# A two-block transformer kernel on one core: the way from the first layer norm into the experts is rewritten

## The chip, the cores and the metric

One core of a Trainium2 chip runs the whole program in one launch. The metric is the device time of one execution in microseconds (us). Engines: PE multiplies matrices (PEld is its weight load), DVE and ACT do elementwise work, POOL is a slower elementwise engine, and SP only issues DMA transfers. Each engine runs its own instructions in order; semaphores tie them together.

## What is computed

Two stacks of two layers each over 256 tokens of width 1024, all in float32. A layer of the first stack is token mixing (three branches with gates), a layer norm, a mixture of 16 experts of which each token uses two, and a second layer norm. Only the piece between the mixing and the experts, and the first expert pair, are touched:

```python
x = layer_norm(DN_ALPHA * x + mix, ln1_g[l], ln1_b[l])
ffn = moe(x.reshape(B * S, D), w_router, router_bias, w1[l], w3[l], w2[l])
x = layer_norm(DN_ALPHA * x + ffn, ln2_g[l], ln2_b[l])
# route: scores = sigmoid(x2 @ w_router); two experts of the best group of four per token;
# gate weight = the two scores, divided by their sum
# an expert: h = silu(xb @ w1[e]) * (xb @ w3[e]);  y = h @ w2[e]
```

The second stack (attention of three kinds and a feed-forward layer) isn't touched.

## The kernel before

The 256 tokens lie as two tiles of 128 partitions (b = 0, 1), each 1024 wide and worked on as two halves of 512 (h = 0, 1). Experts are taken in eight pairs (p = 0 to 7); an expert has 64 slots (CAP), and a one-hot matrix (`sel`) made from each token's rank gathers tokens into slots by matmul. The weights stream through a ring of slots of 1 MB: a pair takes four slots each of w1, w3 and w2, each slot two transfers of 512 KB. `pair_weights` issues them on SP in program order, and a transfer starts when its slot is free and the last one on its semaphore has landed.

The way in, per layer (`first_mix`, end, and `moe`, beginning): `residual` adds the mixing result and takes statistics; `columns` transposes x on PE for the router; `logits` multiplies by router weights into which the norm is folded; `ln_stats` (L503 on) makes mean and `rs` = (var + eps)^-0.5, with both steps after `bn_aggr` on POOL. The norm is applied in three steps per half tile: `center` on DVE, `scale` on ACT, `add` on POOL. `route` turns the logits into scores (tanh on ACT), picks experts in a chain of some twenty small DVE instructions that ends in the mask `rsel` (L855), and counts ranks on PE. `scaled` starts the accumulators of the expert output with ALPHA * x on PE. `gate_weights` normalises the gates after the ranks.

The first pair's gather takes x itself, in float32, with every second column as one weight load, so that the columns match w1 and w3 as they were loaded: partition p holds rows 2p and 2p+1, in one run of 4 KB. The other pairs gather from `xs`: x in three bfloat16 thirds, made by `thirds` (L959 on) after the branch: ACT writes a third, DVE subtracts it from x, three rounds for two tiles. ACT reads x in order there and writes at a step of 256 bytes.

Between the first gather and the first pair's matmuls stands a branch (`tc.If(n > CAP)`, L1058): a path for experts with more than 64 tokens, which this input doesn't take. Every engine loads the largest count and jumps over the path's code. `tc.mark_branch_hint_location` names no engines here, and the built program holds no hint.

What sets the order: PE, DVE and ACT keep the written order between `order.__enter__()` in `first_mix` and `order.__exit__` before the branch, and PE keeps it again through the eight pairs. What stands outside, as `thirds` and `rows_of`, is placed by the scheduler where it fits; it puts the first round of `thirds` on ACT ahead of the branch.

Of the kernel before, what the change touches and what calls it, by code (L numbers as in the profile page):

```python
# [20 lines left out]
NB = 2  # L21
# [19 lines left out]
class Kernel:  # L41
# [458 lines left out]
    def ln_stats(self, st, b):  # L500

        nc = self.nc
        if b == 0:  # L503
            self.mv = self.t(self.cp, [P, NB, 2], F32, "bmv", 2)
            self.rs = self.t(self.cp, [P, NB], F32, "brs", 2)
        mv, rs = self.mv[:, b], self.rs[:, b:b + 1]
        nc.vector.bn_aggr(mv, st)
        nc.gpsimd.tensor_scalar(mv[:, 1:2], mv[:, 1:2], 1e-5, None, OP.add)
        nc.gpsimd.tensor_tensor(rs, mv[:, 1:2], self.half, OP.pow)
        return mv[:, 0:1], rs  # L510

# [32 lines left out]
    def first_mix(self, l, x, mem):  # L544
# [97 lines left out]
        def halves(h, b):  # L642
            return x[:, b, h * 512:h * 512 + 512]
# [19 lines left out]
            nc.vector.scalar_tensor_tensor(halves(h, b), halves(h, b), norms[b][0],  # L663
                                           g[:, h * 512:h * 512 + 512], OP.subtract, OP.mult)

        def scale(h, b):
            nc.scalar.activation(halves(h, b), halves(h, b), AF.Copy, scale=norms[b][1])

        def add(h, b):
            nc.gpsimd.tensor_tensor(halves(h, b), halves(h, b), bb[:, h * 512:h * 512 + 512], OP.add)  # L670

        pss, = self.dense_tok((mh, ml), [ws[0]])
        for b in range(NB):
# [5 lines left out]
        with tc.high_priority(offset=300):  # L679
            residual(1, 0, pss[0])  # L680
            columns(1, 0)
            norms.append(self.ln_stats(st[0], 0))
            for h in range(2):
                center(h, 0)
                scale(h, 0)
                add(h, 0)
        acc = [self.psd() for _ in range(4)]

        def scaled(b, h):
# [4 lines left out]
        order.__enter__()  # L694
        residual(1, 1, pss[1])
        logits(0, 0)
        logits(0, 1)
        columns(1, 1)
        norms.append(self.ln_stats(st[1], 1))
        logits(1, 0)  # L700
        logits(1, 1)
        for h in range(2):
            center(h, 1)
        scaled(0, 0)
        scale(0, 1)
        add(0, 1)
        lgs = self.t(self.cp1, [P, NB, NE], F32, "logits", 1)
        for b in range(NB):
            nc.vector.scalar_tensor_tensor(lgs[:, b], lg[:, b], norms[b][1], self.wb[:, l], OP.mult, OP.add)
        self.M_.__exit__(None, None, None)  # L710
        self.wp_.__exit__(None, None, None)
        return list(pre.values()), (acc, lgs), (scale, add, scaled), order

    def value_weights(self, l):

# [30 lines left out]
    def pair_weights(self, l, p, part, n):  # L746


        w = self.I[part]
        r = self.slot()  # L750
        for a in range(2):
            rows = w[l, 2 * p + a]
            self.nc.sync.dma_start(r[:, a], rows[n * P:(n + 1) * P].rearrange("p (k f) -> p k f", k=2)
                                   if part == "w2" else
                                   rows[2 * n * P:2 * (n + 1) * P].rearrange("(p k) f -> p k f", k=2))
        return r

    def expert_weights(self, l, p, part):
# [62 lines left out]
    def route(self, logits, E, aside):  # L821

        nc = self.nc
        sh = [P, NB, NE]
        sc = self.t(E, sh, F32, "rsc", 1)
        nc.scalar.activation(sc, logits, AF.Tanh, scale=0.5)
        aside()
        bi = self.t(E, sh, F32, "rbi", 1)
        nc.vector.scalar_tensor_tensor(bi, sc, 0.5, self.rbias[:, None, :].to_broadcast(sh),
                                       OP.mult, OP.add)  # L830

        b4 = bi.rearrange("p b (g e) -> p (b g) e", g=4)
        pr = self.t(E, [P, NB * 4, 6], F32, "rpr", 1)
        nc.vector.tensor_tensor(pr[:, :, 0:3], b4[:, :, 0:3], b4[:, :, 1:4], OP.add)
        nc.vector.tensor_tensor(pr[:, :, 3:5], b4[:, :, 0:2], b4[:, :, 2:4], OP.add)
        nc.vector.tensor_tensor(pr[:, :, 5:6], b4[:, :, 0:1], b4[:, :, 3:4], OP.add)
        gs, best = self.gs, self.best
        nc.vector.tensor_reduce(gs[:, :, 0:4], pr.rearrange("p (b g) e -> p b g e", b=NB), AX.X, OP.max)
        nc.vector.tensor_reduce(best[:, :, 0:1], gs[:, :, 0:4], AX.X, OP.max)
        for b in range(NB):  # L840
            nc.vector.match_replace(gs[:, b], best[:, b], gs[:, b], -NEG)

        g4 = bi.rearrange("p b (g e) -> p b g e", g=4)
        for b in range(NB):
            nc.vector.scalar_tensor_tensor(g4[:, b], gs[:, b, 0:4, None].to_broadcast([P, 4, 4]), NEG,
                                           g4[:, b], OP.add, OP.add)
        m8 = [self.t(E, [P, 8], F32, "rm8", 2) for _ in range(NB)]
        for b in range(NB):
            nc.vector.max(m8[b], bi[:, b])
        for b in range(NB):  # L850
            nc.vector.memset(m8[b][:, 2:8], 1.0e30)
        for b in range(NB):
            nc.vector.match_replace(bi[:, b], m8[b], bi[:, b], -3.0e38)
        sel = self.t(E, sh, BF16, "rsel", 1)
        nc.vector.tensor_scalar(sel, bi, -2.0e38, None, OP.is_lt)  # L855

        pk = self.psa()
        nc.tensor.matmul(pk[:, 0:16], self.tri, sel[:, 0], start=True, stop=True)
        nc.tensor.matmul(pk[:, 16:32], self.ones, sel[:, 0], start=True, stop=False)
        nc.tensor.matmul(pk[:, 16:32], self.tri, sel[:, 1], start=False, stop=True)  # L860
        nc.tensor.matmul(pk[:, 32:48], self.ones, sel[:, 0], start=True, stop=False)
        nc.tensor.matmul(pk[:, 32:48], self.ones, sel[:, 1], start=False, stop=True)
        rk = self.t(E, sh, F32, "rrk", 1)
        nc.vector.scalar_tensor_tensor(rk, pk[:, 0:32].rearrange("p (b e) -> p b e", b=NB), 1.0, sel,
                                       OP.add, OP.mult)
        return sc, sel, rk, pk

    def gate_weights(self, sc, sel, pk, E):
        nc = self.nc
        sh = [P, NB, NE]  # L870
        most = self.t(E, [P, 1], F32, "rmost", 1)
        nc.vector.tensor_reduce(most, pk[:, 32:48], AX.X, OP.max)
        most_i = self.t(E, [P, 1], I32, "rmosti", 1)
        nc.vector.tensor_copy(most_i, most)
        nc.vector.tensor_scalar(sc, sc, 0.5, 0.5, OP.mult, OP.add)
        G = self.t(E, sh, F32, "rG", 1)
        nc.vector.tensor_tensor(G, sc, sel, OP.mult)
        gsum = self.t(E, [P, NB], F32, "rgsum", 1)
        nc.vector.tensor_reduce(gsum, G, AX.X, OP.add)
        nc.vector.reciprocal(gsum, gsum)  # L880
        nc.vector.tensor_tensor(G, G, gsum[:, :, None].to_broadcast(sh), OP.mult)
        return G, most_i

    def overflow(self, l, x, acc, rk, G, E):

# [33 lines left out]
    def moe(self, l, x, pre):  # L919
# [5 lines left out]
        self.R3_ = tc.tile_pool(name=f"raw3_{l}", bufs=1, reuse_waits="tile")  # L925
        self.R3 = self.R3_.__enter__()
        with tc.tile_pool(name=f"moe{l}", bufs=1, reuse_waits="tile") as E:
            pre, (acc, logits), (scale, add, scaled), order = pre
            def aside():

                scale(1, 1)
                add(1, 1)
                scaled(0, 1)
                scaled(1, 0)

            sc, sel, rk, pk = self.route(logits, E, aside)

            def slots(p, dt=BF16):

# [18 lines left out]
            def thirds():  # L958

                xs = self.t(E, [P, 3, NB, 8, P], BF16, "xs", 1)  # L960
                for i in range(3):
                    for b in range(NB):
                        to = xs[:, i, b].rearrange("p (n k) c -> p n c k", k=2)
                        xb = x[:, b].rearrange("p (n c k) -> p n c k", k=2, c=P)
                        nc.scalar.copy(to, xb)  # L965
                        if i < 2:
                            nc.vector.tensor_tensor(xb, xb, to, OP.subtract)
                return [lambda b, k, i=i: xs[:, i, b, k] for i in range(3)]

            def rows_of():  # L970

                t = self.t(E, [P, NB, 7, NE], BF16, "rt", 1)
                nc.vector.memset(t[:, :, 1:4], 0.0)
# [3 lines left out]
                nc.vector.tensor_tensor(rest, G, t[:, :, 4], OP.subtract)  # L977
                nc.vector.tensor_copy(t[:, :, 5], rest)
                nc.vector.tensor_tensor(t[:, :, 6], rest, t[:, :, 5], OP.subtract)
                id16 = self.t(E, [P, P], BF16, "id16", 1)  # L980
                nc.scalar.copy(id16, self.ident)
                ps = self.psa()
# [63 lines left out]

            mT = mv = None
            label = f"few{l}"
            tc.mark_branch_hint_location(label, "LikelyTaken")
            s = slots(0, F32)  # L1050
            scaled(1, 1)
            xk = x.rearrange("p b (n c k) -> p b n k c", k=2, c=P)
            g_ = gather(s, [lambda b, k: xk[:, b, k // 2, k % 2]])
            order.__exit__(None, None, None)
            G, most = self.gate_weights(sc, sel, pk, E)
            nxt = [self.expert_weights(l, 1, n) for n in ("w1", "w3")]
            n = nc.values_load(most[0:1, 0:1], min_val=0, max_val=S)
            with tc.If(n > CAP, label=label):  # L1058
# [5 lines left out]
            for p in range(8):  # L1064
# [8 lines left out]
                    g, bb = self.ln_rows(I["ln2_g"][l], I["ln2_b"][l])  # L1073
                sl = hidden(w, g_)
                if p == 0:
                    rows, pick = rows_of()
                if p < 7:
                    g_ = gather(slots(p + 1), parts)
                elif l < DEPTH - 1:
                    mT = self.mem_T(mem)  # L1080
                sT, gsl = back(p)
# [553 lines left out]
```

## Time and profile before

| | us |
|---|---|
| Three runs | 1663.26, 1670.53, 1671.15 (median 1670.53) |
| The profiled execution, its own time | 1663.95 |
| Its span in the trace | 1662.2 |
| PE busy | 1589.8 (96%) |
| DVE, ACT, POOL busy | 869.2, 741.2, 105.9 |

PE is busy nearly throughout, so the whole follows PE: what counts is where PE stands idle, and how fast it goes where its clock isn't granted in full. DVE and ACT are busy half the time, and matter where PE waits for them.

### The profile page before, as it was taken

How to read it: one execution, taken by the hardware profiler on the slowest of the kernel's cores; microseconds unless marked ns; L12 is line 12 of the kernel's file. 1: busy time of each engine (PE TensorE's matmuls, PEld its weight loads, DVE VectorE, ACT ScalarE, POOL GpSimd, SP SyncE). 2: the span in 40 equal slices, each digit the busy share in tenths (PEclk: the TensorE clock that was granted, in tenths of full speed). 3: DMA queues.
4: the chain of work that ended last, by engine and by line, in shares of the span. 5: the costliest groups of instructions: out<-in, count | busy, mean ns of one | idle time of the engine just before them, and what ended most of it. 6: DMA issues, size and time to landing. Idle time of an engine off the chain costs nothing.

```text
span 1662.2 us, 24843 instructions
## 1 busy us (share of the span) xinstructions
PE 1589.8 (96%) x9844; PEld 1191.6 (72%) x9844; DVE 869.2 (52%) x1778; ACT 741.2 (45%) x1186; POOL 105.9 (6%) x141
## 2 busy tenths in 40 slices
PE   7999999799999999999799998989999999899999
PEld 7877998434345987998444443866989987688897
DVE  5586547311123688547421213777655568775554
ACT  5546445610103555544710102656555556655553
POOL 0000013000000000012100000130000000200000
PEclk9999999899999999999899999999999999999999
DMA  9553867699999653686699998623555554145551
GB/s 309 178 171 102 324 235 250 248 372 409 409 408 376 204 165 117 257 299 228 223 377 409 409 409 326 236 93 104 170 185 175 180 163 168 52 161 194 178 184 45
DMA packets 158470, 394.78 MB, mean 238 GB/s; under 512 B 15716, under 2 KB 21860, under 8 KB 158340
## 3 DMA queue, kind: packets, MB, share of 16 engines
q1 hardware_dynamic: 153088, 384.98, 63.6%
q0 software_dynamic: 2144, 6.91, 1.3%
q8 instruction: 80, 1.31, 0.3%
q10 hardware_dynamic: 3108, 1.16, 0.3%
q14 instruction: 50, 0.41, 0.1%
HBM read 391.97 MB, written 1.05 MB: 236 GB/s over the span
## 4 chain that ended last, share of the span: by engine, by line
PE 41%; DVE 4%; ACT 2%; POOL 1%; DMA 1%; issue 1%; ACTq 0%; DVEq 0%; POOLq 0%
PE a L1010 6%; PE d L113 6%; PE d L112 6%; PE d L111 6%; PE a L111 4%; PE a L112 4%; PE a L113 4%; PE a L1031 3%; DMA raw<-in_w_in_dram 1%; PE a L954 1%; DVE wl L105 1%; ACT xs L965 1%; PE d L1044 1%; PE a L386 0%; PE a L381 0%
## 5 line engine op out<-in xcount | busy, mean ns | idle before, releaser
L100 DVE TENSOR_TENSOR wl<-raw,wh 128x1024 fp32r<-128x1024 f32 (+1 forms) x232 | 283.8, 1225 | 215.7 <-ACT wh L99 212.2
L99 ACT CAST wh<-raw 128x1024 fp32r<-128x1024 f32 (+1 forms) x232 | 240.2, 1038 | 239.8 <-PE d L112 133.7
L111 PE MATMUL d<-big,wh 128*128 128x256 f32 (+1 forms) x976 | 277.7, 285 | 2.0 <-ACT big L176 1.1
L112 PE MATMUL d<-big,wh 128*128 128x256 f32 (+1 forms) x976 | 277.2, 284 | 2.1 <-DVE big L177 2.1
L113 PE MATMUL d<-big,wl 128*128 128x256 f32 (+1 forms) x976 | 275.7, 284 | 0.0
L1010 PE MATMUL a<-raw,xg 128*64 128x512 f32 x832 | 185.5, 601 | 7.7 <-DVEq L1058 7.7
L105 DVE SCALAR_TENSOR_TENSOR wl<-raw,gcols,wh 128x512 fp32r<-128x512 f32 (+1 forms) x224 | 151.5, 711 | 77.7 <-ACT wh L104 77.4
L104 ACT ACTIVATE wh<-raw,gcols 128x512 fp32r<-128x512 f32 (+1 forms) x224 | 143.5, 686 | 104.1 <-PE a L113 38.8
L111 PEld LDWEIGHTS d<-big,wh 128*128 128x128 f32 (+1 forms) x976 | 186.1, 191 | 5.2 <-ACT big L176 1.8
L112 PEld LDWEIGHTS d<-big,wh 128*128 128x128 f32 (+1 forms) x976 | 186.1, 191 | 4.8 <-DVE big L177 2.6
L111 PE MATMUL d<-wh,big 128*128 128x512 f32 (+1 forms) x480 | 186.9, 390 | 0.0
L113 PE MATMUL d<-wh,big 128*128 128x512 f32 (+1 forms) x480 | 186.7, 390 | 0.2 <-DVE big L177 0.2
L112 PE MATMUL d<-wl,big 128*128 128x512 f32 (+1 forms) x480 | 185.5, 387 | 1.1 <-DVE wl L105 0.9
L113 PEld LDWEIGHTS d<-big,wl 128*128 128x128 f32 (+1 forms) x976 | 185.7, 191 | 0.4 <-issue 0.3
L1010 PEld LDWEIGHTS a<-raw,xg 128*64 128x64 f32 x832 | 61.6, 139 | 126.8 <-issue 118.5
L1015 DVE TENSOR_TENSOR sl<-sl,a 128x512 f32<-128x512 f32 x16 | 11.0, 687 | 191.5 <-PE a L1010 171.9
L1031 PE MATMUL a<-raw,sl 128*64 128x512 f32 x480 | 107.0, 595 | 0.7 <-ACT sl L1022 0.7
L113 PEld LDWEIGHTS d<-wh,big 128*128 128x128 f32 x480 | 91.6, 191 | 18.5 <-issue 1.5
L111 PEld LDWEIGHTS d<-wh,big 128*128 128x128 f32 x480 | 91.7, 191 | 17.5 <-issue 1.8
L112 PEld LDWEIGHTS d<-wl,big 128*128 128x128 f32 x480 | 91.5, 191 | 17.5 <-DVE wl L105 1.5
L111 PE MATMUL a<-wh,s 128*128 128x512 f32 x256 | 101.3, 396 | 0.0
L112 PE MATMUL a<-wl,s 128*128 128x512 f32 x256 | 101.2, 395 | 0.0
(417 smaller groups left out, 2313.2 us busy)
## 6 DMA issues: line engine op xcount, KB each, us to landing
raw<-in_w_dram SPq DMA_DIRECT2D x328, 512.0 KB, 10.2
raw<-in_w_in_dram SPq DMA_DIRECT2D x64, 1024.0 KB, 5.5
raw<-in_w_ff_dram SPq DMA_DIRECT2D x64, 1024.0 KB, 5.4
br<-in_w_dram SPq DMA_DIRECT2D x36, 512.0 KB, 8.9
raw<-in_w_out_dram SPq DMA_DIRECT2D x16, 1024.0 KB, 5.1
raw<-in_w_br_dram SPq DMA_DIRECT2D x12, 1024.0 KB, 6.2
raw<-in_w_mem_kv_dram SPq DMA_DIRECT2D x7, 1024.0 KB, 12.6
gate<-in_w_dram SPq DMA_DIRECT2D x12, 512.0 KB, 10.2
```

What stands on the lines that cost most here:

```text
L99: nc.scalar.copy(hi, src)
L100: nc.vector.tensor_tensor(lo, src, hi, OP.subtract)
L104: nc.scalar.activation(hi[:, k], src[:, k], AF.Copy, scale=g)
L105: nc.vector.scalar_tensor_tensor(lo[:, k], src[:, k], g, hi[:, k], OP.mult, OP.subtract)
L111: mm(ps, sh, mh, start=start, stop=False)
L112: mm(ps, sh, ml, start=False, stop=False)
L113: mm(ps, sl, mh, start=False, stop=stop)
L954: mm(ps[:, kk], part(b, k + kk), s[:, b], start=(i == 0), stop=(i == len(terms) - 1))
L965: nc.scalar.copy(to, xb)
L1010: mm(ps[64 * a:64 * a + 64], g_[:, k, 64 * a:64 * a + 64], w[i][k // 2][:, a, k % 2], start=(k == 0), stop=(k == 7))
L1031: mm(pss[h][64 * a:64 * a + 64], hT[:, k, 64 * a:64 * a + 64], w[k][:, a, h], start=(k == 0), stop=(k == 3))
L1044: mm(acc[2 * b + h], sT[:, b * P:b * P + P], ys[h][:, i], start=False, stop=(p == 7 and i == 1))
```

## The change

- `ln_stats`: the step that adds eps moves from POOL to DVE; the power stays on POOL. All four kinds of norm call use it, two layers with two norms each.
- The norm's second step: `scale` (ACT) and `add` (POOL) become one DVE instruction, `normed`; both halves of tile 0 run before tile 1's residual, the last half of tile 1 in `aside`.
- `columns(1, 1)` and the statistics of tile 1 move ahead of `logits(0, 1)`.
- `route` normalises the gates before it takes the ranks; the largest count is taken after the one-hot matrix; the parts for `rows_of` and the second pair's one-hot matrix are written out before the branch.
- `thirds`: ACT writes each third contiguously and reads x at a step of 8 bytes; DVE reads and writes x at that step. The first pair's w1 and w3 are loaded with the rows p and 128+p of a block on a partition (two runs of 2 KB), so that its gather takes contiguous columns of x.
- The hint is asked for in layer 0 alone, on all five engines.

```diff
         nc.vector.bn_aggr(mv, st)
-        nc.gpsimd.tensor_scalar(mv[:, 1:2], mv[:, 1:2], 1e-5, None, OP.add)
+        nc.vector.tensor_scalar(mv[:, 1:2], mv[:, 1:2], 1e-5, None, OP.add)
...
-        def scale(h, b):
-            nc.scalar.activation(halves(h, b), halves(h, b), AF.Copy, scale=norms[b][1])
-
-        def add(h, b):
-            nc.gpsimd.tensor_tensor(halves(h, b), halves(h, b), bb[:, h * 512:h * 512 + 512], OP.add)
+        def normed(h, b):
+            nc.vector.scalar_tensor_tensor(halves(h, b), halves(h, b), norms[b][1],
+                                           bb[:, h * 512:h * 512 + 512], OP.mult, OP.add)
...
         logits(0, 0)
-        logits(0, 1)
         columns(1, 1)
         norms.append(self.ln_stats(st[1], 1))
+        logits(0, 1)
...
+                                   rows[2 * n * P:2 * (n + 1) * P]
+                                   .rearrange("(p k) f -> p k f" if p else "(k p) f -> p k f", k=2))
...
-                        to = xs[:, i, b].rearrange("p (n k) c -> p n c k", k=2)
-                        xb = x[:, b].rearrange("p (n c k) -> p n c k", k=2, c=P)
+                        to = xs[:, i, b].rearrange("p (n k) c -> p n k c", k=2)
+                        xb = x[:, b].rearrange("p (n c k) -> p n k c", k=2, c=P)
                         nc.scalar.copy(to, xb)
                         if i < 2:
                             nc.vector.tensor_tensor(xb, xb, to, OP.subtract)
...
-            tc.mark_branch_hint_location(label, "LikelyTaken")
+            if l == 0:
+                tc.mark_branch_hint_location(label, "LikelyTaken",
+                                             {EN.PE, EN.DVE, EN.Activation, EN.SP, EN.Pool})
             s = slots(0, F32)
             scaled(1, 1)
-            xk = x.rearrange("p b (n c k) -> p b n k c", k=2, c=P)
-            g_ = gather(s, [lambda b, k: xk[:, b, k // 2, k % 2]])
+            most = self.most(pk, E)
+            rt = parted()
+            s1 = slots(1)
+            g_ = gather(s, [lambda b, k: x[:, b, k * P:(k + 1) * P]])
             order.__exit__(None, None, None)
-            G, most = self.gate_weights(sc, sel, pk, E)
```

On ACT, in layer 0 between the last transposed columns (`big`) and the branch, the order before was:

```order
L655 COPY big_2785<-a_2970 128x4x128
L965 CAST xs_7623<-x_78 128x4x128x2
L667 ACTIVATE x_78<-x_78,brs_2944 128x512
L826 ACTIVATE rsc_3003<-logits_2992 128x32
L667 ACTIVATE x_78<-x_78,brs_2944 128x512
L981 CAST id_1666_7681<-ident 128x128
L989 CAST pick_7688<-k_323 128x1024
L965 CAST xs_7623<-x_78 128x4x128x2
L1057 TENSOR_LOAD rmosti_3066
```

And the same place in the changed program (L824 is the tanh of the scores, L963 the third):

```order
L655 COPY big_2785<-a_2964 128x4x128
L963 CAST xs_7634<-x_78 128x1024
L983 CAST id_1667_7684<-ident 128x128
L991 CAST pick_7691<-k_323 128x1024
L824 ACTIVATE rsc_3000<-logits_2989 128x32
L963 CAST xs_7634<-x_78 128x1024
L1062 TENSOR_LOAD rmosti_3052
```

The two scalings are gone, the first third still stands ahead of the tanh, and two constant casts have moved ahead of it too.

On DVE, in layer 0 from the mask `rsel` to the first pair's one-hot matrix (`sel`), before:

```order
L855 TENSOR_SCALAR rsel_3029<-rbi_3009 128x32
L877 TENSOR_TENSOR rG_3069<-rsc_3003,rsel_3029 128x32
L879 TENSOR_REDUCE rgsum_3071<-rG_3069 128x2
L864 SCALAR_TENSOR_TENSOR rrk_3037<-a_3031,rsel_3029 128x32
L872 TENSOR_REDUCE rmost_3064<-a_3031 128x1
L942 TENSOR_TENSOR sel_549_3039<-k_316,rrk_3037 128x256
```

And now (`rrk` are the ranks, `rG` and `rgsum` the gates and their sums):

```order
L853 TENSOR_SCALAR rsel_3025<-rbi_3005 128x32
L861 TENSOR_SCALAR rsc_3000<-rsc_3000 128x32
L863 TENSOR_TENSOR rG_3034<-rsc_3000,rsel_3025 128x32
L865 TENSOR_REDUCE rgsum_3036<-rG_3034 128x2
L866 RECIPROCAL rgsum_3036<-rgsum_3036 128x2
L867 TENSOR_TENSOR rG_3034<-rG_3034,rgsum_3036 128x32
L869 SCALAR_TENSOR_TENSOR rrk_3040<-a_3027,rsel_3025 128x32
L940 TENSOR_TENSOR sel_551_3047<-k_316,rrk_3040 128x256
```

Three more gate instructions stand between the mask and the ranks, and the reduction to the largest count has moved behind `sel`.

At the program's start, here DVE's first instructions, the difference is:

```order
@@ -1,3 +1,4 @@
-L1631 UNCONDITIONAL_BRANCH
+L1636 UNCONDITIONAL_BRANCH
+L1636 BRANCH_PREFETCH_HINT
 L211 MEMSET ones 128x128
 L246 MEMSET halfpi 128x1
```

The hint has been moved to the very start of the program, on each engine, hundreds of instructions ahead of the branch that it belongs to; there is none for layer 1.

## Rows read from the trace of the kernel before

**Rows 1.** Waits of PE, whole run: waiter, releaser: us, times, longest.

```profile
PE a L1010 <- DVEq L1058: 7.7, 2, 3.9
PE a L954 <- ACT xs L965: 7.0, 2, 3.6
PE a L174 <- POOL x L524: 6.5, 1, 6.5
```

**Rows 2.** Timeline of layer 0's way in: start, length, instruction, [idle before <- releaser].

```profile
280.81 1.41 DVE L663 SCALAR_TENSOR_TENSOR x<-x,bmv,gate 128x512 f32<-128x512 f32 x2
...
285.73 1.99 PE L659 MATMUL a<-wrg,big 128*128 128x16 f32 x16
...
286.41 4.73 ACT L965 CAST xs<-x 128x1024 bf16<-128x1024 f32 x1
...
287.83 0.38 DVE L709 SCALAR_TENSOR_TENSOR logits<-a,brs,wrb 128x16 f32<-128x16 f32 x2 [0.61 <-PE a L659]
...
291.45 0.23 ACT L826 ACTIVATE rsc<-logits 128x32 f32<-128x32 f32 x1
...
291.65 2.48 POOL L670 TENSOR_TENSOR x<-x,gate 128x512 f32<-128x512 f32 x2 [4.00 <-ACT x L667]
291.71 1.25 DVE L829 SCALAR_TENSOR_TENSOR rbi<-rsc,rbias 128x32 f32<-128x32 f32 x1 [3.45 <-ACT rsc L826]
...
292.99 1.18 DVE L834 TENSOR_TENSOR rpr<-rbi 128x24 f32<-128x24 f32 x1
...
296.07 0.18 DVE L855 TENSOR_SCALAR rsel<-rbi 128x32 bf16<-128x32 f32 x1
...
296.46 2.06 PE L691 MATMUL d<-x,k 128*128 128x512 f32 x2
...
298.31 5.17 PE L954 MATMUL a<-sel,x 128*128 128x128 f32 x32
...
307.13 2.36 DVE L967 TENSOR_TENSOR x<-x,xs 128x1024 f32<-128x1024 f32 x2 [2.93 <-DVEq L1058]
...
307.29 13.93 PE L1010 MATMUL a<-raw,xg 128*64 128x512 f32 x56 [3.82 <-DVEq L1058]
```

**Rows 3.** Page, costliest groups: instructions, forms, count | us in all, mean ns | idle before.

```profile
L99 ACT CAST wh<-raw 128x1024 fp32r<-128x1024 f32 (+1 forms) x232 | 240.2, 1038 | 239.8 <-PE d L112 133.7
```

**Rows 4.** Timeline of layer 0, from the first pair to the second pair's gather.

```profile
322.88 0.32 PE L984 MATMUL a<-id,rt 128*112 128x128 bf16 x2
...
331.95 0.66 PE L1021 MATMUL a<-ident,sl 128*128 128x128 f32 x4
...
333.28 1.94 PE L1031 MATMUL a<-br,sl 128*64 128x512 f32 x8 [0.68 <-ACT sl L1022]
```

**Rows 5.** Timeline of PE over later pairs of layer 0.

```profile
340.20 12.19 PE L1010 MATMUL a<-raw,xg 128*64 128x512 f32 x56
...
354.03 2.85 PE L954 MATMUL a<-sel,xs 128*128 128x128 bf16 x48
...
357.24 0.66 PE L1021 MATMUL a<-ident,sl 128*128 128x128 f32 x4
...
380.45 2.85 PE L954 MATMUL a<-sel,xs 128*128 128x128 bf16 x48
```

**Rows 6.** Timeline of layer 1: its first gather.

```profile
805.24 4.38 PE L954 MATMUL a<-sel,x 128*128 128x128 f32 x32
```

**Rows 7.** The branch's line, PE's sequencer: ns min/median/max, first and last start.

```profile
L1058 PEldq COMPARE_BRANCH  x2: 3332/3438/3543, 301.8 to 807.8; - x2
```

**Rows 8.** The gathers' line, weight loads of x at 8-byte steps: ns min/median/max.

```profile
L954 PEld LDWEIGHTS a<-sel,x x64: 196/197/337, 297.5 to 809.2; 128*128 128x128 f32 x64
```

**Rows 9.** Stretches: length, busy by engine (count), granted clock, DMA share, GB/s.

```profile
307.00:311.00 4.00, 3.71 (x10) 1.31 (x12) 2.36 (x2) 2.61 (x1) 0.00 (x0) 0.61 0.00 2
480.00:490.00 10.00, 10.00 (x85) 5.40 (x82) 2.36 (x4) 0.03 (x1) 0.00 (x0) 1.00 1.02 409
```

**Rows 10.** Timeline of POOL at layer 1's end, tile 1's statistics.

```profile
1035.63 0.60 POOL L508 TENSOR_SCALAR bmv<-bmv 128x1 f32<-128x1 f32 x1 [0.79 <-DVE bmv L507]
```

More of the change, by code (lines that the diff above doesn't have):

```diff
@@ L684, in first_mix @@
                 center(h, 0)
-                scale(h, 0)
-                add(h, 0)
+            for h in range(2):
+                normed(h, 0)
         acc = [self.psd() for _ in range(4)]
@@ L703, in first_mix @@
             center(h, 1)
+        normed(0, 1)
         scaled(0, 0)
-        scale(0, 1)
-        add(0, 1)
         lgs = self.t(self.cp1, [P, NB, NE], F32, "logits", 1)
@@ L711, in first_mix @@
         self.wp_.__exit__(None, None, None)
-        return list(pre.values()), (acc, lgs), (scale, add, scaled), order
+        return list(pre.values()), (acc, lgs), (normed, scaled), order
     def value_weights(self, l):
@@ L754, in pair_weights @@
                                    if part == "w2" else
-                                   rows[2 * n * P:2 * (n + 1) * P].rearrange("(p k) f -> p k f", k=2))
+                                   rows[2 * n * P:2 * (n + 1) * P]
+                                   .rearrange("(p k) f -> p k f" if p else "(k p) f -> p k f", k=2))
         return r
@@ L862, in route @@
         nc.tensor.matmul(pk[:, 32:48], self.ones, sel[:, 1], start=False, stop=True)
[L863 to L874, printed above, removed]
         nc.vector.tensor_scalar(sc, sc, 0.5, 0.5, OP.mult, OP.add)
@@ L881, in gate_weights, with most @@
         nc.vector.tensor_tensor(G, G, gsum[:, :, None].to_broadcast(sh), OP.mult)
-        return G, most_i
+        rk = self.t(E, sh, F32, "rrk", 1)
+        nc.vector.scalar_tensor_tensor(rk, pk[:, 0:32].rearrange("p (b e) -> p b e", b=NB), 1.0, sel,
+                                       OP.add, OP.mult)
+        return G, rk, pk
+    def most(self, pk, E):
+        nc = self.nc
+        most = self.t(E, [P, 1], F32, "rmost", 1)
+        nc.vector.tensor_reduce(most, pk[:, 32:48], AX.X, OP.max)
+        most_i = self.t(E, [P, 1], I32, "rmosti", 1)
+        nc.vector.tensor_copy(most_i, most)
+        return most_i
     def overflow(self, l, x, acc, rk, G, E):
@@ L927, in moe @@
         with tc.tile_pool(name=f"moe{l}", bufs=1, reuse_waits="tile") as E:
-            pre, (acc, logits), (scale, add, scaled), order = pre
+            pre, (acc, logits), (normed, scaled), order = pre
             def aside():
-                scale(1, 1)
-                add(1, 1)
+                normed(1, 1)
                 scaled(0, 1)
                 scaled(1, 0)
-            sc, sel, rk, pk = self.route(logits, E, aside)
+            G, rk, pk = self.route(logits, E, aside)
             def slots(p, dt=BF16):
@@ L968, in thirds, with parted @@
                 return [lambda b, k, i=i: xs[:, i, b, k] for i in range(3)]
-            def rows_of():
+            def parted():
                 t = self.t(E, [P, NB, 7, NE], BF16, "rt", 1)
@@ L979, in rows_of @@
                 nc.vector.tensor_tensor(t[:, :, 6], rest, t[:, :, 5], OP.subtract)
+                return t
+            def rows_of(t):
                 id16 = self.t(E, [P, P], BF16, "id16", 1)
@@ L1075, in moe @@
                 if p == 0:
-                    rows, pick = rows_of()
+                    rows, pick = rows_of(rt)
                 if p < 7:
-                    g_ = gather(slots(p + 1), parts)
+                    g_ = gather(slots(p + 1) if p else s1, parts)
                 elif l < DEPTH - 1:
```

## The prediction, as it went on record

> **What bounds the kernel now.** I read the page's first parts (PE is busy 96% of the span), then the waits of PE, then the timeline around each wait. PE is the bound, so the change can only give back what PE loses in the stretches it touches. The list of waits has three entries there [rows 1]: after the branch PE waits for DVE's sequencer, 7.7 us in two layers; the second pair's gather (L954) waits for ACT's thirds, 7.0 in two layers; at layer 1's end the first matmul of the next stack waits 6.5 for a POOL step. To these come waits on the way to the first gather and the slow stretch behind each idle time: the timeline of layer 0 shows the chain logits (L659, L709), tanh (L826), mask (L829 to L855), gather (L954), first pair (L1010) [rows 2]. The profiled execution took 1663.95 us, 1.75 more than its span of 1662.2, and 6.6 less than the median of the three runs. The sum is made on the 1663.95.
>
> **Scores earlier.** Before, the logits are done on DVE at 287.83 + 0.38 = 288.21, but the tanh starts only at 291.45, because ACT's first third, written at a step of 256 bytes, holds it from 286.41 to 291.14, with one scaling behind it [rows 2]. Now that third is written in order and read at a step of 8 bytes. The nearest row for ACT's 128x1024 cast in order is 1.04 us [rows 3]; the dearest is the 4.73 itself. Reads at 8-byte steps are shown on PE, whose weight loads of x go at that step in 196 ns for 128 columns [rows 8], so I take 1.04. The third and two constant casts (which I put at 1.4 together) then end before the tanh is due. Four of the eight logits matmuls of tile 0 move behind the transposes: half of L659's 1.99, 1.0 us later, against transposes that start some 0.55 earlier, so the scores are done 0.45 later, at about 288.7. On DVE one `normed` (0.70, half of L663's 1.41 for two) goes ahead of L709, where DVE stood idle for 0.61: nothing more. Tanh at 288.75 instead of 291.45: gain 2.7.
>
> **The mask's chain alone.** L829 and L834 take 1.25 and 1.18 on 32 and 24 columns, beside POOL's add of 2.48 that starts in the same 0.1 us; L855, on 32 columns after POOL is done, takes 0.18 [rows 2]. Without POOL's add the two cost 0.4 together: 2.05 less. Against it, half of one more `normed` stands ahead of them, 0.4. Net 1.65; bounds 0.95 (a whole `normed`) and 2.05. With the 2.7 the mask ends 4.35 earlier, in each layer.
>
> **Gates ahead of the ranks.** Three more small DVE instructions and the scaling stand between mask and ranks, 0.2 each, at most 0.8 later. Before, PE starts the gather 2.06 after the mask because `scaled(1, 1)` holds it (296.46 to 298.3, mask end 296.25) [rows 2]; with ranks, `sel` and four instructions more I count 1.85 from mask to `sel`. Cost 0, bounds -0.3 and 0.6; once PE's cover is gone it is the 0.6. The largest count, the seven parts for `rows_of` and the second one-hot matrix, about ten instructions of 0.2 to 0.38, stand behind `sel` while PE takes 5.17 for the gather [rows 2]: 0, at most 1.
>
> **Gather.** 5.17 in layer 0 [rows 2], 4.38 in layer 1 [rows 6]. Less idle time stands ahead of it; I take 0.5 in each, between 0 and the 0.8 by which the two differ.
>
> **First pair's weights.** Runs of 2 KB instead of 4. PE's waits name no transfer at L1010 [rows 1], so there is slack: 0. If these 8.4 MB took twice as long as at 409 GB/s [rows 9] and nothing covered that, it would be 20.5 once per layer.
>
> **Branch.** Every engine leaves its stream here. PE's sequencer spends 3.3 and 3.5 us in the compare-and-branch [rows 7]; DVE stands 2.93 and PE 3.82 before the first pair [rows 2]. If a hint makes the target ready, about 0.95 of PE's time is left: gain 2.85, layer 0 alone, as layer 1 has no hint before or after. [...]
>
> **Thirds in time.** From the `rows_of` transposes at 322.88 to the second pair's down matmuls at 333.28 go 10.40 us [rows 4]. Without the wait: 0.3 for the transposes, 3.21 from gather to L1021 as in the next pair (354.03 to 357.24) [rows 5], 1.33 from L1021 to L1031 [rows 4], 4.8 in all: gain 5.6, and the same in layer 1, which has half of the 7.0 [rows 1]. After the branch the chain was 1.2 for one subtract and four thirds at 4.73, 20.1; it becomes four subtracts at 1.18 and a third, about 6, when more than 15 are given. A new cost s of the subtract at 8-byte steps: nearest row 1.18, where it read the third at 256-byte steps [rows 2]; far bound twice ACT's 4.73, since it reads and writes that way.
>
> [...]
>
> **End of layer 1 and the rest.** POOL's add of eps takes 0.60 after an idle 0.79 [rows 10], and tile 0's stands in the same queue ahead of the step that PE waits 6.5 for [rows 1]. On DVE it is 0.2. Gain 1.0, bounds 0 and 1.9. Early in each layer DVE takes over eps and `normed` of tile 0, where it waits for PE: 0, at most 0.5 later.
>
> **Sum.** Layer 0: 4.35 + 0.5 + 2.85 + 1.74 + 5.6 = 15.0. Layer 1: 4.35 + 0.5 + 5.6 = 10.5. End: 1.0. Together 26.5: 1637.5 on the profiled execution's scale, 1644 on the median's. I forecast 1640, between the two, since executions of before stand at both levels.
>
> **Rivals.**
> (a) The hint does nothing. It stands at the start of the program, hundreds of instructions ahead of its branch. [...] For it: the distance. Against it: nothing in the trace, where no hint was ever run. [...]
> (b) Transfers become the bound. A pair moves twelve slots of 1.05 MB, 12.6 MB, which takes 30.8 us at the 409 GB/s of a stretch with the DMA full [rows 9]; PE's pair takes 380.45 - 354.03 = 26.4 [rows 5]. So the queue loses 4.4 a pair on PE, and PE's lead, loaded ahead, may run out earlier when PE gains 6 to 13 us after the branch. [...]
> (c) ACT's cost lies in the step itself, read or written. The third stays at 4.73, the tanh comes at about 292.1, 0.65 later than before instead of 2.7 earlier, and the thirds are as late as before: 26.5 - 6.7 - 11.2 = 8.6, 1655. Against it: PE's 196 ns.
> (d) Slower: DVE pays for reading and writing x at the 8-byte step. The thirds are then ready 4s + 1 after the branch instead of 20.1, and that wait is PE's. Up to s = 4.8 it is no longer than before; from 6.7 the other 7.6 per layer are gone, from 7.7 the kernel is over 0.5% slower, at s = 9.5 the wait is 18.9 longer in each layer, +22.5 net: 1686. For it: ACT loses a factor of 4.5 on a step. Against it: DVE read the same steps at 1.18.
>
> **How the numbers follow.** Forecast 0.55, (a) 0.25, (b) 0.07, (c) 0.08, (d) 0.05. A measurement of this kernel can tell about 0.5%, 8.3 us, from no change. The first three and half of (c) are faster than that, a half of (c) lies within, with a little of (b); (d) is slower: 0.86, 0.09, 0.05. Range 1630 to 1658: the low end is the forecast on the lower scale with the bounds of the mask (0.4), gather (0.3), gates (0.3), each twice, the end (0.9) and about 4 for what follows each idle time at a lower clock that I did not book; the high end takes in (a), (b) and (c) with the scale of the median.
>
> **What would show it.** Right: ACT's thirds at about 1.0 each and the tanh at about 2.7 us earlier against the logits; its successors at 0.2 instead of 1.2; one wait for the branch of 3.9 in PE's list instead of two; no wait of L954 for the thirds; 56 records of layer 0's first pair in 12.2; no POOL add of eps. Wrong: two waits for the branch (a); waits of L1010 or L1031 for weights, at later pairs (b); thirds at 4.7 (c); subtracts of 5 or more (d); a gather that starts more than 2.1 after the mask.

## The result and the profile after

The kernel before ran at a median of 1667.6 us (four runs), the changed kernel at 1642.87 (four runs, 1637.66 to 1645.47): ratio 0.9849 with a 95% interval of 0.981 to 0.9888. The profiled execution took 1641.19, 22.8 less than the profiled one of before; the forecast had 26.5 on that scale and 1640 as the time.

The waits of PE over the whole run, after (waiter, releaser: us, times, longest):

```profile
PE a L174 <- POOL x L524: 5.3, 1, 5.3
PE a L1012 <- DVEq L1063: 5.3, 2, 3.7
```

Of the three entries in [rows 1] the thirds are gone, the branch's (now L1063) fell from 7.7 to 5.3, nearly all of it in layer 0, and POOL's from 6.5 to 5.3. To compare places, both traces need a common mark ahead of the change: PE's transposes of tile 0 (L654). Before, in layer 0 and layer 1 (start, length):

```profile
279.86 0.66 PE L654 MATMUL a<-ident,x 128*128 128x128 f32 x4
...
786.76 0.66 PE L654 MATMUL a<-ident,x 128*128 128x128 f32 x4
...
803.00 0.18 DVE L855 TENSOR_SCALAR rsel<-rbi 128x32 bf16<-128x32 f32 x1
...
813.50 13.70 PE L1010 MATMUL a<-raw,xg 128*64 128x512 f32 x56 [3.88 <-DVEq L1058]
...
828.84 0.32 PE L984 MATMUL a<-id,rt 128*112 128x128 bf16 x2
...
839.06 1.94 PE L1031 MATMUL a<-br,sl 128*64 128x512 f32 x8 [0.67 <-ACT sl L1022]
...
1038.60 1.75 PE L174 MATMUL a<-ident,x 128*128 128x128 f32 x7 [6.50 <-POOL x L524]
```

After, layer 0's way in, the rows that answer to [rows 2 to 4]:

```profile
281.20 0.66 PE L654 MATMUL a<-ident,x 128*128 128x128 f32 x4
...
286.32 3.46 PE L659 MATMUL a<-wrg,big 128*128 128x16 f32 x24
...
287.00 1.13 ACT L963 CAST xs<-x 128x1024 bf16<-128x1024 f32 x1
...
289.61 5.47 PE L689 MATMUL d<-x,k 128*128 128x512 f32 x6
289.81 0.38 DVE L706 SCALAR_TENSOR_TENSOR logits<-a,brs,wrb 128x16 f32<-128x16 f32 x2 [0.90 <-PE a L659]
...
290.22 0.23 ACT L824 ACTIVATE rsc<-logits 128x32 f32<-128x32 f32 x1 [0.95 <-DVE logits L706]
...
290.77 0.18 DVE L827 SCALAR_TENSOR_TENSOR rbi<-rsc,rbias 128x32 f32<-128x32 f32 x1
...
290.99 0.18 DVE L832 TENSOR_TENSOR rpr<-rbi 128x24 f32<-128x24 f32 x1
...
293.07 0.18 DVE L853 TENSOR_SCALAR rsel<-rbi 128x32 bf16<-128x32 f32 x1
...
294.87 0.22 PE L856 MATMUL a<-rsel,tri 128*128 128x16 bf16 x1
...
296.03 3.81 PE L952 MATMUL a<-sel,x 128*128 128x128 f32 x32
...
301.23 4.84 DVE L965 TENSOR_TENSOR x<-x,xs 128x1024 f32<-128x1024 f32 x4 [0.66 <-DVEq L1063]
301.39 12.24 PE L1012 MATMUL a<-raw,xg 128*64 128x512 f32 x56 [1.55 <-DVEq L1063]
...
315.27 0.32 PE L986 MATMUL a<-id,rt 128*112 128x128 bf16 x2
...
319.96 1.94 PE L1033 MATMUL a<-br,sl 128*64 128x512 f32 x8 [0.68 <-ACT sl L1024]
```

And layer 1 with its end, after:

```profile
773.76 0.66 PE L654 MATMUL a<-ident,x 128*128 128x128 f32 x4
...
784.94 0.18 DVE L853 TENSOR_SCALAR rsel<-rbi 128x32 bf16<-128x32 f32 x1
...
786.79 3.81 PE L952 MATMUL a<-sel,x 128*128 128x128 f32 x32 [0.37 <-DVE rmost L877]
794.34 15.11 PE L1012 MATMUL a<-raw,xg 128*64 128x512 f32 x56 [3.74 <-DVEq L1063]
...
811.10 0.32 PE L986 MATMUL a<-id,rt 128*112 128x128 bf16 x2
...
815.78 1.94 PE L1033 MATMUL a<-br,sl 128*64 128x512 f32 x8 [0.68 <-ACT sl L1024]
...
1013.96 1.33 PE L174 MATMUL a<-ident,x 128*128 128x128 f32 x5 [5.29 <-POOL x L524]
```

Layer 0 starts 281.20 - 279.86 = 1.34 later than before, and its second pair's down matmuls stand at 319.96 instead of 333.28: 13.32 + 1.34 = 14.7 gained in between (forecast 15.0). Layer 1 starts 13.00 earlier, and the same place is 839.06 - 815.78 = 23.28 earlier: 10.3 (forecast 10.5). The end brings 24.64 - 23.28 = 1.4 (forecast 1.0). Together 26.3, against 26.5. The whole time gained 3.5 less: 1.3 is lost ahead of layer 0, 0.3 between the two places measured in the layers, 1.9 behind the first stack. The largest pieces are stretches of lower granted clock. The first window is before, the other four after (length, then busy time and count of PE, PEld, DVE, ACT and POOL, then granted clock, DMA share, GB/s):

```profile
42.00:46.00 4.00, 3.27 (x27) 3.27 (x28) 1.28 (x3) 0.45 (x1) 0.00 (x0) 1.00 0.02 4
```

```profile
42.00:46.00 4.00, 3.18 (x15) 3.18 (x16) 1.36 (x4) 0.00 (x0) 0.00 (x0) 0.52 0.02 4
289.00:295.00 6.00, 6.00 (x13) 2.71 (x14) 4.04 (x29) 1.61 (x3) 0.00 (x0) 0.50 1.01 373
795.00:800.00 5.00, 5.00 (x14) 1.58 (x12) 3.90 (x4) 4.42 (x4) 0.00 (x0) 0.50 0.19 45
1090.00:1097.00 7.00, 5.82 (x18) 4.45 (x20) 3.66 (x8) 3.17 (x6) 1.60 (x4) 0.52 0.00 0
```

The low one of the two at 42 costs about 1.0 of the 1.3 ahead of layer 0; the one at 1090 costs about as much as the 1.9 after the first stack. Nothing in the edit explains these two. The stretches at 289 and 795 lie inside the changed code and are taken up below.

### The profile page after: what moved, and what is told of

Its sections match the earlier page's. It is cut to its first block, busy times and chain, and to the rows that moved or that the text cites. A ratio compares the mean times of both kernels' runs of the same rounds, so it can differ in the third digit from the quotient of the medians.

```text
span 1639.4 us, 24826 instructions
## 1 busy us (share of the span) xinstructions
PE 1586.0 (97%) x9844; PEld 1189.4 (73%) x9844; DVE 870.7 (53%) x1794; ACT 694.8 (42%) x1178; POOL 91.7 (6%) x125
## 3 DMA queue, kind: packets, MB, share of 16 engines
q8 instruction: 79, 1.29, 0.3%
q10 hardware_dynamic: 3108, 1.16, 0.3%
## 4 chain that ended last, share of the span: by engine, by line
PE 43%; DVE 4%; POOL 1%; DMA 1%; ACT 1%; issue 1%; ACTq 0%; DVEq 0%; POOLq 0%
PE a L1012 7%; PE d L113 6%; PE d L112 6%; PE d L111 6%; PE a L111 4%; PE a L112 4%; PE a L113 4%; PE a L1033 3%; PE a L952 1%; DVE wl L105 1%; DMA raw<-in_w_in_dram 1%; PE d L1046 1%; DVE sall L1358 1%; PE a L386 0%; PE a L381 0%
```

## Experiments

**No hint.**

```diff
-            if l == 0:
-                tc.mark_branch_hint_location(label, "LikelyTaken",
-                                             {EN.PE, EN.DVE, EN.Activation, EN.SP, EN.Pool})
+            tc.mark_branch_hint_location(label, "LikelyTaken")
```

> The changed kernel with no hint in either layer. Theory (the hint arms the jump of layer 0's branch): layer 0's first pair of experts waits for the branch about 3.7 us as layer 1 does, PE's compare-and-branch takes 3.3 to 3.6 us in both layers instead of 0.39 in layer 0, the 56 matmuls of that pair take 13.7 to 15 instead of 12.2 because the clock falls after the idle time, and the whole is 4 to 5 us slower than the changed kernel (about 1647). Rival (the short wait of layer 0 came from the earlier arrival of the engines, not from the hint): the wait stays at about 1.5 us and the time at about 1643.

Measured 1645.64, ratio 0.9858 (0.9834 to 0.9881). PE's compare-and-branch (ns, min/median/max over the two layers), and layer 0's first pair:

```profile
L1061 PEldq COMPARE_BRANCH  x2: 3357/3474/3592, 298.1 to 797.1; - x2
```

```profile
303.45 12.24 PE L1012 MATMUL a<-raw,xg 128*64 128x512 f32 x56 [3.82 <-DVEq L1061]
```

The hint makes the short wait: without it both layers stall again, and layer 0's first pair starts 2.06 later. One part of the expectation failed: the clock didn't fall behind this wait, and the 56 matmuls took 12.24. The granted clock was 1.00 over 303.5 to 315.5. So the loss is 2 to 3 us, less than expected, and the whole times can't tell it: the intervals of the two ratios overlap.

**Both hints at the start.** The condition `if l == 0` is dropped.

> The changed kernel with the hint asked for in both layers; both hints come to stand at the start of the program, one behind the other. Theory (an engine holds one hint, the later one replaces the earlier): layer 0's wait is back at about 3.7 us with a compare-and-branch of over 3 us, layer 1's falls to about 1.5 with 0.4; the sum about as the changed kernel, 1640 to 1646. Rival 1 (each branch keeps its own hint): both short, about 5 us faster, 1638. Rival 2 (a hint doesn't last over hundreds of microseconds and another branch): both long, 1647.

Measured 1643.64, ratio 0.9854 (0.983 to 0.9877).

```profile
L1062 PEldq COMPARE_BRANCH  x2: 388/1918/3447, 298.5 to 788.9; - x2
```

The short one is layer 0's, as in the changed kernel: PE waits 1.55 there and 3.55 in layer 1. So only one of the two hints held, and the expectation named the wrong layer. In the built program layer 1's hint stands first and layer 0's second; the trace shows two hints on each engine within the first microsecond, but not which is which. By that order the later one held, or the one for the nearest branch; no run here tells these two apart. Layer 1's branch wasn't served by its hint at the start, so the next two runs put one behind layer 0's branch.

**A hint in time.** In layer 1's `first_mix`, behind `columns(1, 1)` (`self.n0` is layer 0's largest count, kept from its branch):

```diff
+        if l == 1:
+            self.tc.mark_branch_hint_location("few1", self.n0 > CAP, {EN.PE, EN.DVE, EN.Activation, EN.SP})
```

> The changed kernel with a second hint, for layer 1, whose outcome is taken from a register of layer 0's count, so that it stands between layer 0's branch and layer 1's branch (on PE, DVE, ACT and SP, a few microseconds ahead of layer 1's branch). Theory: layer 1's wait for the branch falls from 3.74 to about 1.5 us, its first pair from 15.1 to 12.2, and layer 0 stays as it is: 5 us faster than the changed kernel, about 1638. Rival (the hint must be far ahead): layer 1 unchanged, about 1643, or slower by the register step.

Measured 1640.3, ratio 0.9829 (0.9806 to 0.9852). The branch on PE in both layers, and what stands behind layer 1's branch:

```profile
L1066 PEldq COMPARE_BRANCH  x2: 347/370/393, 297.8 to 788.5; - x2
```

```profile
793.84 2.36 DVE L967 TENSOR_TENSOR x<-x,xs 128x1024 f32<-128x1024 f32 x2 [2.93 <-DVEq L1066]
```

PE's stall is gone in both layers, but DVE still stands 2.93 at layer 1's branch, and PE waits for its copies as before. So DVE's stall, not PE's, was the last to end. The hint stood on both engines at 778.1, which is 10.4 us ahead of the branch on PE and 12.5 us, some 40 instructions, ahead of it on DVE; on DVE it was no use. The theory's 5 us didn't come: PE waits 3.81 where the changed kernel waits 3.74, and the whole time differs by no more than the runs can tell.

**A hint far ahead**, in layer 0's fourth pair, behind its one-hot matrices on DVE:

```diff
-                    g_ = gather(slots(p + 1) if p else s1, parts)
+                    with tc.manual_schedule(engines={EN.DVE}):
+                        s2 = slots(p + 1) if p else s1
+                        if l == 0 and p == 3:
+                            tc.mark_branch_hint_location("few1", self.n0 > CAP, {EN.PE, EN.DVE, EN.SP})
+                    g_ = gather(s2, parts)
```

> The changed kernel with layer 1's hint asked for in layer 0's fourth pair of experts, some 400 of DVE's instructions and 400 us ahead of layer 1's branch (PE, DVE and SP), where the run before had it 40 instructions ahead on DVE and DVE still stood 3.0 us at the branch. Theory (DVE's hint came too late in its stream): DVE's idle time behind layer 1's branch falls from 3.0 to about 0.6 us, PE's wait from 3.7 to about 1.5, the first pair's 56 matmuls take 12.2 to 13.7 instead of 15.1; 2 to 5 us faster than the changed kernel, 1636 to 1640. Rival (a hint taken from a register does nothing on DVE): DVE 3.0 again, 1640 to 1643.

Measured 1635.41, ratio 0.9814 (0.9794 to 0.9834), the lowest median of all kernels here; its interval still overlaps that of the changed kernel, so the gain is shown by the trace and not by the whole time. Layer 1:

```profile
789.48 4.84 DVE L965 TENSOR_TENSOR x<-x,xs 128x1024 f32<-128x1024 f32 x4 [0.41 <-DVEq L1064]
...
789.63 12.24 PE L1012 MATMUL a<-raw,xg 128*64 128x512 f32 x56 [1.29 <-DVEq L1064]
```

DVE's idle time fell to 0.41, PE's to 1.29, the first pair from 15.11 to 12.24. Together that is 5.3 us, where the forecast gave layer 0's hint 4.6.

**Thirds written at the old step**, in the changed kernel:

```diff
-                        to = xs[:, i, b].rearrange("p (n k) c -> p n k c", k=2)
-                        xb = x[:, b].rearrange("p (n c k) -> p n k c", k=2, c=P)
+                        to = xs[:, i, b].rearrange("p (n k) c -> p n c k", k=2)
+                        xb = x[:, b].rearrange("p (n c k) -> p n c k", k=2, c=P)
```

> The changed kernel with the thirds written at a step of 256 bytes again (x read in order). Theory (ACT pays for the step of its writes): each third takes 4.7 us, the tanh comes 3 us later in both layers, the second pair's gather waits for the thirds again, 10.4 us instead of 4.7 from the transposes of the rows to the second pair's down matmuls: 14 to 18 us slower than the changed kernel, 1657 to 1661. Rival (layer 0's end is set by the transfers, which have no lead left in the changed kernel's last pair): layer 0 loses less, since its weights come no later, and the whole is 8 to 11 us slower, 1651 to 1654.

Measured 1659.68, ratio 0.9954 (0.9935 to 0.9973): 17 slower than the changed kernel, as the theory has it. Part of that is a stretch of lower clock (0.50 to 0.60 from 624 to 635 us) that no part of the edit explains. PE's wait for the thirds is back, here in layer 0 and then in layer 1; the changed kernel has none:

```profile
PE a L952 <- ACT xs L963: 4.9, 2, 4.2
...
PE a L952 <- ACT xs L963: 3.4, 1, 3.4
```

Layer 0's way in:

```profile
284.77 3.59 PE L659 MATMUL a<-wrg,big 128*128 128x16 f32 x24
...
285.45 4.73 ACT L963 CAST xs<-x 128x1024 bf16<-128x1024 f32 x1
...
291.13 0.23 ACT L824 ACTIVATE rsc<-logits 128x32 f32<-128x32 f32 x1
...
295.55 2.69 PE L952 MATMUL a<-sel,x 128*128 128x128 f32 x22 [0.36 <-DVE rmost L877]
```

Counted from L659, the tanh comes 2.46 later than in the changed kernel, but the gather only 1.07. In layer 1 they come 3.2 and 3.2 later. So in layer 0 the early tanh was mostly not on the path.

**Thirds alone**, the same two lines the other way in the kernel before.

> The kernel before with one part of the change alone: the thirds written in order, x read and written at a step of 8 bytes. Theory: no wait of the second pair's gather for the thirds (5.6 us in each layer), and the tanh about 2.7 us earlier, of which POOL's add, now earlier too, may take back a part: 14 to 17 us faster than before, ratio 0.990 to 0.9915. Rival (the weights of layer 0's last pairs, which land 1.8 us ahead of PE at the least, come to bound it): about 4 less, ratio 0.9925.

Measured 1650.61, ratio 0.9899 (0.9879 to 0.9919): 16.8 of the 25 us come from these two lines. POOL and DVE behind the tanh:

```profile
288.20 2.49 POOL L670 TENSOR_TENSOR x<-x,gate 128x512 f32<-128x512 f32 x2 [0.83 <-ACT x L667]
288.31 1.21 DVE L829 SCALAR_TENSOR_TENSOR rbi<-rsc,rbias 128x32 f32<-128x32 f32 x1 [0.24 <-ACT rsc L826]
...
289.55 1.18 DVE L834 TENSOR_TENSOR rpr<-rbi 128x24 f32<-128x24 f32 x1
```

DVE is held up here too, where POOL's add and the tanh both come earlier; it is not the tanh's lateness.

**POOL's add back**, in the changed kernel, for the last half tile:

```diff
         def normed(h, b):
+            if h == b == 1:
+                nc.scalar.activation(halves(h, b), halves(h, b), AF.Copy, scale=norms[b][1])
+                nc.gpsimd.tensor_tensor(halves(h, b), halves(h, b), bb[:, h * 512:h * 512 + 512], OP.add)
+                return
```

> The changed kernel, but the last half of tile 1 is scaled on ACT and added to on POOL as in the kernel before, behind the tanh. Theory (POOL's add holds up DVE's small instructions): the two DVE instructions that run beside POOL's add take about 1.2 us instead of 0.19, the mask ends about 1.5 us later against the logits (0.7 of `normed` saved, 2.0 lost), and layer 1's gather starts later by as much; layer 0's by less, since PE is busy there until the ranks. Rival (they were long for another reason, as their first read of the tanh's result): they stay at 0.19.

One run, 1644.09. The two instructions stayed at 0.19, as the rival had it, but for a reason neither named: with one scaling only, POOL's add started behind them. Another pair ran beside it:

```profile
289.72 1.26 POOL L669 TENSOR_TENSOR x<-x,gate 128x512 f32<-128x512 f32 x1 [2.85 <-ACT x L668]
289.91 0.16 DVE L841 TENSOR_REDUCE best<-gs 128x2 f32<-128x8 f32 x1
...
290.33 0.15 DVE L843 MATCH_REPLACE8 gs<-best,gs 128x8 f32<-128x8 f32 x1
290.39 0.70 DVE L847 SCALAR_TENSOR_TENSOR rbi<-gs,rbi 128x16 f32<-128x16 f32 x2
```

In the changed kernel the same two (L843 there) take 0.29, and end when POOL isn't busy. Here the reduction and the replacement ran at their usual 0.16 and 0.15 in the middle of POOL's add, and the first instruction with two tensors as inputs (L847) ended only behind the add's own end at 290.98. (MATCH_REPLACE8 is counted here as reading one tensor: a MATCH_VALUE_LOAD of its own, 0.08 to 0.09, stands ahead of each.) Layer 1 shows the same: 0.16 and 0.15 beside a POOL add of 1.26, and 0.70 for L847's two. That DVE's two-tensor instructions are the ones that wait is what these rows show; why they do isn't shown.

**Ranks ahead of the gates**: the gates' five instructions behind the largest count.

> The changed kernel with the gates normalised behind the largest count, not ahead of the ranks. Theory (PE's own queue sets the gather in layer 0, DVE's chain in layer 1): layer 0's gather starts as before, 2.8 us behind the mask's end; layer 1's, which waits 0.37 for DVE, starts about 0.4 earlier, 1.3 behind the mask's end. Rival (the gates' place costs its whole 0.8): both start 0.8 earlier. In the whole time nothing that a single run can tell.

One run, 1640.96. The gather starts 1.84 and 1.85 behind the mask's end, directly behind `scaled` and with no wait for DVE. The expectation had 2.8 and 1.3, so both numbers missed. Layer 0's 1.84 is 0.94 less than in the changed kernel, as the rival would have it, but the gates' place isn't what shortened it: from the ranks to the gather it is 1.11, in the changed kernel 1.16. The clock fell later here, so that the six `scaled` matmuls took 4.52 instead of 5.47 and the ranks came sooner behind the mask. The clock was low at `scaled` in both layers of this run, so PE's queue set both, and layer 1's 0.4 could not show. With the hint far ahead as well:

> The changed kernel with layer 1's hint from layer 0's fourth pair and the gates normalised behind the largest count. Theory: as the run with the hint far ahead, but for 0.4 us in layer 1, where the gather waits for DVE: 1634.5 to 1636. Rival (the gates ahead of the ranks cost their 0.8 in both layers): 1633.5 to 1634.

Measured 1637.23, ratio 0.9817 (0.9793 to 0.984): no difference from the 0.9814 without this edit that the runs can tell. But in this run's trace layer 0 has the full clock at `scaled` (2.82 for the six), and there the 0.4 does show, mask and gather:

```profile
289.58 0.18 DVE L853 TENSOR_SCALAR rsel<-rbi 128x32 bf16<-128x32 f32 x1
...
290.94 3.81 PE L956 MATMUL a<-sel,x 128*128 128x128 f32 x32
```

The gather starts 1.18 behind the mask's end and waits for nothing; in the changed kernel's layer 1, at the same clock, it is 1.67 with a wait for DVE. So the gates' place costs 0.5 where the clock is full, nothing where it is low, and the rival's 0.8 in neither.

**What the rest is worth**: the kernel before with the new thirds and both hints.

> The kernel before with the thirds written in order and both hints (layer 0's at the program's start, layer 1's from layer 0's fourth pair): without the norm's step on DVE, the order of logits and gates, and eps on DVE. Theory (those other edits give 1 to 1.6 us in layer 1, 1.4 at layer 1's end and nothing in layer 0, where PE's own queue sets the gather): 2.5 to 4 us slower than the run with the hint far ahead, 1638 to 1640. Rival (they are worth the 1.65 per layer of the prediction's mask chain and the 1.0 of the end, and gather's 1 us): 5 to 6 slower, 1641. Rival 2 (they are worth nothing): 1635 to 1636.

Measured 1640.16, ratio 0.9845 (0.9828 to 0.9862), 4.8 slower than the run with the hint far ahead, between the theory and its rival; the intervals of the two ratios overlap a little. In the traces 1.4 of it is layer 1's end, where PE's wait for POOL is 6.49 instead of 5.32; the rest is the way in of both layers, where the two runs' clocks fell at different places, so it can't be divided further. The norm on DVE, eps on DVE, the new order and the first pair's layout are worth about a fifth of the thirds and hints.

## Why the prediction was right, step by step

- **Scores and mask.** The mask ends 4.34 earlier in layer 0 (forecast 4.35), the two DVE instructions are at 0.18. Thirds alone took 4.8 from the tanh to the mask's end, the changed kernel 3.0: 1.7 for POOL's add, forecast 1.65. The mechanism holds. That layer 0 meets the number to 0.01 is luck: in layer 1, where the router's matmuls had the full clock (1.00 instead of 0.77, 24 of L659 in 2.75 instead of 3.46), the mask ends 5.06 earlier, 0.7 more than forecast.
- **Mask to gather, forecast at no cost: wrong in layer 0.** The gather starts 296.03 - 293.25 = 2.78 behind the mask, not 1.85. PE isn't held by DVE but by its own queue: the granted clock was 0.50 over 289 to 295, the six `scaled` matmuls took 5.47 and the ranks stand behind them, 1.6 after the mask. Of the 4.34 only 3.62 reached the gather. The step asked who waits for DVE, not whether PE would still be free once DVE was faster. The prediction's own sign of being wrong, a gather more than 2.1 behind the mask, came true here. In layer 1, at the full clock (1.00 over 781.50 to 784.32, the six in 2.82), it was 1.67. So the loss hangs on where the clock falls, and that differs from run to run: in the last run of Ranks ahead of the gates, layer 0 had the full clock and PE stood 0.86 waiting for the mask.
- **Gather.** 3.81 in both layers, so 1.36 and 0.57 saved where 0.5 was taken: the bound of 0.8 was too tight, because the clock was full again by then (1.00, where before it was 0.73 over layer 0's gather, 298.31 to 303.48, and 0.89 over layer 1's, 805.24 to 809.62). A part that the sum didn't have is the layout: with the old one, Thirds alone took 4.01 in both layers, behind two `scaled` matmuls of 1.10, which is their time at a clock of 1.00 (785.32 to 786.42 in the changed kernel), so contiguous columns save 0.2.
- **Branch.** Right that the hint works over hundreds of instructions: rival (a) is out. The stall that it counted on is there without a hint (3.36 and 3.59 on PE in No hint) and gone with one (0.39). The 0.95 that the sum left to PE was an estimate with no row behind it; 1.55 is left. So the gain was 3.82 - 1.55 = 2.27, not 2.85, because PE waits for DVE, and DVE's own jump still costs 0.66. So PE's list counts two waits, 3.74 and 1.55, where the prediction had one.
- **Clock behind the idle time.** The sum's 1.74, for layer 0 alone, is the 13.93 of its 56 matmuls [rows 2] less the 12.19 of the second pair's [rows 5]. 13.93 fell to 12.24, 1.69 where 1.74 was forecast, with the clock at 1.00 over the 56 (301.39 to 313.63), where before it was 0.88 over them. Over all runs the 56 matmuls took 12.24 behind each of the twelve waits of 1.3 to 1.6, and 13.55 to 15.20 behind eleven of the twelve of 3.5 to 4.1; behind the twelfth, layer 0's without the hint, they took 12.24. So a long wait nearly always costs 1.3 to 3.0 more. Layer 1's 15.11 cost 1.4 that the sum didn't have, and its way in gave 1.1 more.
- **Thirds in time.** 10.40 fell to 4.69, in layer 1 10.22 to 4.68: 5.7 and 5.5, forecast 5.6. ACT's third takes 1.13 and DVE's subtract 1.21 at 8-byte steps, so (c) and (d) are out.
- **Transfers, (b).** They came to the point of mattering. In layer 0's last pair PE's weight load waits:

```profile
497.83 0.62 PEld L1012 LDWEIGHTS a<-raw,xg 128*64 128x64 f32 x5 [0.44 <-DMA raw<-in_w_dram]
```

An ordinary gap there is 0.28. From the last pair's first matmul to the transposes behind it (L174) it is 14.45 (485.24 to 499.69), against 13.84 before: 0.6 in one layer, not the 12.9 (the 1.74 and both layers' 5.6) that would be back if the transfers were the bound. In the last run of Ranks ahead of the gates, whose way into layer 0 was 2.3 shorter, a weight load of that pair waits 1.06 and the same stretch is 15.08; in the run before it, with a way in 1.7 shorter, the stretch is 14.19. So the transfers can take back a part of a further gain in layer 0; how much, no run here settles.
- **End.** 1.36 for 1.0, inside its bounds.

The mechanisms were right, but that the total came out within 0.2 is luck: optimistic steps (mask to gather, -0.7; branch, -0.6; layer 1's clock, -1.4) stood beside cautious ones (gather, +0.9; layer 1's way in, +1.1; the end, +0.4).

## What to carry to other kernels

When a chain on one engine is shortened, work out what the waiting engine has in its own queue in that time, at the clock that it has there: that queue is the next bound (here six `scaled` matmuls of 5.47 us at a clock of 0.50). Write in order and let the reader take the step, where the step of the writes is the one that costs, as on ACT here (4.73 us a third against 1.13). A hint for a jump needs its place in the stream checked on every engine, as the slowest engine's stall is the one that is paid: in A hint in time PE's compare-and-branch took 0.35 us, and PE still waited 3.81 for DVE.

## What the runs showed that was not expected

- A hint at the program's start still served a branch some 297 us later: 0.39 us for PE's compare-and-branch instead of 3.3 to 3.6. On DVE a hint some 40 instructions (12.5 us) ahead did nothing, one some 400 (420 us) ahead took the idle time from 2.93 to 0.41; on PE one 10.4 us ahead brought the compare-and-branch to 0.35. Whether distance or time decides wasn't tried.
- The step costs ACT when it writes (4.73 against 1.13), not DVE when it reads the same tile (1.18 before, 1.21 now with an 8-byte step on both sides). What ACT would pay to read at 256 bytes isn't shown; it read at 8.
- In these traces DVE's instructions with one tensor as input ran at their usual length beside POOL's add (0.16 and 0.15 us); those with two waited until it ended (1.25 and 1.18 instead of 0.18 in the kernel before; 0.70 instead of 0.29 for two in POOL's add back).
